# Half 0's products of six pairs instead of four ahead of the quarter sums, in the up projections of a two-layer trunk

## The chip, the core and the metric

The kernel runs on one core of one Trainium2 chip. The time is device microseconds of that core, the median of several executions; a profiled execution has a time of its own beside its span. The engines are PE (TensorE matmuls; PEld loads their weights beside it), DVE (VectorE), ACT (ScalarE), POOL (GpSimd) and SP (SyncE, which here only issues loads). In the trace each engine works off its instructions in the order in which they stand in the program, so what stands behind a waiting instruction on its engine is late with it.

## The reference, cut to what matters

```python
def squared_relu_mlp(h, w_up, w_down):
    return jnp.square(jax.nn.relu(h @ w_up)) @ w_down

# per layer, x is (1, 1024, 1024), w_up (1024, 4096), all float32
x = x + g_m[:, None, :] * rmsnorm(y, norm_g[l, 1])      # y: conv mixer (layer 0) or attention (layer 1)
h = modulate(rmsnorm(x, norm_g[l, 2]), sh_f, sc_f)
y = squared_relu_mlp(h, mlp_up_w[l], mlp_down_w[l])
x = x + g_f[:, None, :] * rmsnorm(y, norm_g[l, 3])
```

Two layers are computed, so there are two up projections. The change touches the place where the mixer's output projection ends, the residual `x` is written, `h` is formed, and the product `h @ w_up` begins.

## The kernel before, in words

**Numbers.** Each float32 operand is kept as a high part (`uphi`, the first tile of a pair, ACT's copy at L159) and a low part (`uplo`, DVE's subtraction at L160). A product of two such operands is three matmuls into one PSUM bank (`mm`, L156). Every matmul of the up projection is 128 by 128 by 512 tokens.

**The pairs.** The 4096 columns of `w_up` are taken in 16 pairs of 128-column blocks; with the tokens in two halves of 512 and the 1024 inner rows in two halves of four steps, a pair is a 2 by 2 block product, made by seven products instead of eight. Each product is 4 steps of 3 matmuls, 12 in all. On the tokens' side the seven operands are called `11` and `21` (half 0 of the tokens, inner rows 0 to 511 and 512 to 1023), `22` (from half 1), and `t1` to `t4` (sums over quarters of both halves). `11` and `21` need only half 0; the other five need half 1. On the weights' side a pair loads two blocks a and b: `11` and `21` use a as it is, and `pair_sums` (L467 on) forms `t2`, `s2` and `t3` from a and b, splitting each into high and low parts.

**The seam.** `Seam` closes the preceding projection, row tile by row tile: norm, gate, residual, store, norm again. `quarter_steps` then gives two lists. `steps0` holds eight steps for half 0: four transposes on PE into a `tp` bank and ACT's scaling at L374 (the front), then DVE's cast and subtraction at L384 and L385 (the back); they fill `11` and `21`. `steps1` holds four steps for half 1, one per quarter kk: eight transposes and two scalings (the front, `front1`), then the back, `back1`: four subtractions on DVE (L405, L407, L410, L412), five high parts on ACT (L395) and five low parts on DVE (L398). They fill `22` and `t1` to `t4`.

**`first_pairs`** writes by hand the order of work there; inside `with pinned()` each engine keeps the order in which the lines are written. It makes the two products of half 0 for the first AHEAD = 4 pairs (`first`: product 11, copied out of its bank by ACT at L599; `second`: product 21 on top of it, copied out with a Relu at L603), between the fronts and backs of `steps0` and `steps1`, and then the five other products of pair 0, one step kk of all five after the other. The weights of pairs 0 to 2 are split before, that of pair 3 (`late`) within.

**`all_pairs`** makes the other pairs. A pair whose half 0 is done already (called *begun* here: 1 to 3) has five products; any other has seven. Its last two products (`second` and `fourth` there) and the adds behind them are done within the next pair: behind the next pair's product 11 and product 21 if that pair is not begun, behind its first product of `s2` if it is. The second product into a bank has to wait until DVE has added the bank's value to its row (`take`, L528). Here the tile framework's scheduler sets the order on each engine. `sums` (L1124 to L1127) and the stores `ha` follow for each pair, and `load_pair` loads the next blocks into the four tiles of `raw`: a load waits until the tile's last reader, the split of `t3` two pairs before, is through.

## Time and profile before

| what | value |
| --- | --- |
| median of 3 runs (lowest to highest) | 2157.41 us (2154.37 to 2158.88) |
| the profiled execution: own time, span | 2159.2 us, 2157.4 us |
| busy share of the span: PE, DVE, ACT | 96%, 71%, 50% |
| 380 to 400 us: PE busy, granted clock | 17.57 of 20 us, 0.91 |
| 420 to 440 us: PE, DVE busy, granted clock | 14.17 and 18.75 of 20 us, 0.85 |
| 1550 to 1570 us: PE, DVE busy, granted clock | 14.19 and 18.27 of 20 us, 0.91 |

The first seam ends and the first up projection begins at about 385 us, the second at about 1510 us. A timeline row is the start in us, a duration in us, the engine, the line, the operation, output and inputs by name, the count of merged instructions, and in brackets the idle time ahead with what ended it. PE's matmuls are pipelined: one takes 0.39 us and the next starts 0.23 us after it. A waits row is the engine and line that waited, what it waited for, and us in total, times, and the longest.

### The profile page before, as it was taken

How to read it: one execution, taken by the hardware profiler on the slowest of the kernel's cores; microseconds unless marked ns; L12 is line 12 of the kernel's file. 1: busy time of each engine (PE TensorE's matmuls, PEld its weight loads, DVE VectorE, ACT ScalarE, POOL GpSimd, SP SyncE). 2: the span in 40 equal slices, each digit the busy share in tenths (PEclk: the TensorE clock that was granted, in tenths of full speed). 3: DMA queues.
4: the chain of work that ended last, by engine and by line, in shares of the span. 5: the costliest groups of instructions: out<-in, count | busy, mean ns of one | idle time of the engine just before them, and what ended most of it. 6: DMA issues, size and time to landing. Idle time of an engine off the chain costs nothing.

```text
span 2157.4 us, 25064 instructions
## 1 busy us (share of the span) xinstructions
PE 2062.0 (96%) x9438; PEld 1688.2 (78%) x9438; DVE 1541.2 (71%) x2087; ACT 1084.3 (50%) x1533; POOL 5.3 (0%) x13
## 2 busy tenths in 40 slices
PE   4999999989999999999899999999899999999998
PEld 3788878768888788888677788887678888788886
DVE  6877876876665669977688887756875665566576
ACT  4533353745554444455665565555744444544443
POOL 0000000000000000000000000000000000000000
PEclk9999999999999999999999999999999999999999
DMA  7444464254553889656223331143254653774355
GB/s 223 121 138 147 137 205 133 88 184 161 182 181 139 280 292 322 208 166 211 69 70 120 97 96 35 59 135 138 71 185 150 215 180 134 266 252 158 98 175 167
DMA packets 251023, 344.47 MB, mean 160 GB/s; under 512 B 19253, under 2 KB 142482, under 8 KB 250902
## 3 DMA queue, kind: packets, MB, share of 16 engines
q1 hardware_dynamic: 208408, 252.50, 37.4%
q10 hardware_dynamic: 42494, 90.38, 11.3%
q8 instruction: 74, 1.21, 0.2%
q14 instruction: 47, 0.39, 0.1%
HBM read 258.94 MB, written 83.89 MB: 159 GB/s over the span
## 4 chain that ended last, share of the span: by engine, by line
PE 77%; DVE 11%; ACT 6%; DMA 3%; issue 2%; ACTq 0%; SPq 0%; DVEq 0%
PE one L156 42%; PE mm L156 20%; PE tp L156 7%; PE big L156 3%; PE big L1360 2%; ACT junk L271 2%; DVE y L327 1%; PE tp L1386 1%; DVE raw L328 1%; DMA aw<-in_ada_w_dram 1%; ACT slot L1210 1%; DVE av L909 1%; PE tp L433 1%; DVE ring L160 1%; DVE acc L186 1%
## 5 line engine op out<-in xcount | busy, mean ns | idle before, releaser
L156 PE MATMUL one<-slot,uphi 128*128 128x512 f32 x1224 | 377.8, 389 | 0.0
L156 PEld LDWEIGHTS one<-slot,uphi 128*128 128x128 f32 x1224 | 230.4, 188 | 48.3 <-issue 0.5
L156 PE MATMUL one<-ring,ring 128*128 128x512 f32 x1152 | 262.9, 389 | 2.3 <-DVE ring L160 2.3
L160 DVE TENSOR_TENSOR uplo<-raw,uphi 128x1024 fp32r<-128x1024 f32 x127 | 153.3, 1222 | 143.1 <-ACT uphi L159 143.1
L156 PEld LDWEIGHTS one<-ring,ring 128*128 128x128 f32 x1152 | 215.9, 188 | 48.3 <-ACT ring L159 3.1
L156 PE MATMUL one<-slot,uplo 128*128 128x512 f32 x612 | 240.7, 393 | 8.2 <-DVE y L528 3.8
L160 DVE TENSOR_TENSOR ring<-raw,ring 128x1024 fp32r<-128x1024 f32 x144 | 174.3, 1220 | 55.6 <-ACT ring L159 55.3
L159 ACT ACTIVATE ring<-raw 128x1024 fp32r<-128x1024 f32 x144 | 149.5, 1052 | 106.6 <-DMA raw<-ha 61.6
L159 ACT ACTIVATE uphi<-raw 128x1024 fp32r<-128x1024 f32 x127 | 134.7, 1061 | 118.6 <-PE one L156 82.3
L156 PE MATMUL mm<-ring,ring 128*128 128x512 f32 x768 | 185.0, 390 | 1.6 <-DVE ring L160 1.6
L156 PE MATMUL tp<-ring,ring 128*128 128x512 f32 x768 | 183.9, 389 | 0.0
L159 ACT ACTIVATE ring<-w 128x1024 fp32r<-128x1024 f32 x80 | 84.8, 1060 | 178.7 <-PE tp L156 102.7
L156 PEld LDWEIGHTS mm<-ring,ring 128*128 128x128 f32 x768 | 143.7, 188 | 32.1 <-DVE ring L160 2.5
L156 PEld LDWEIGHTS tp<-ring,ring 128*128 128x128 f32 x768 | 144.1, 188 | 29.9
L160 DVE TENSOR_TENSOR ring<-w,ring 128x1024 fp32r<-128x1024 f32 x80 | 97.8, 1222 | 81.1 <-ACT ring L159 81.1
L156 PEld LDWEIGHTS one<-slot,uplo 128*128 128x128 f32 x612 | 115.2, 188 | 35.8 <-DVE y L528 5.5
L186 DVE SCALAR_TENSOR_TENSOR acc<-raw,csil,acc 128x1024 f32<-128x1024 f32 x88 | 112.5, 1278 | 22.8 <-DMA raw<-in_ada_w_dram 18.0
L526 ACT ACTIVATE y<-one 128x512 f32<-128x512 f32 x66 | 39.0, 591 | 159.6 <-PE one L156 118.5
L156 PE MATMUL mm<-slot,uphi 128*128 128x512 f32 x344 | 109.2, 399 | 9.6 <-DVE slot L398 9.4
L156 PE MATMUL one<-slot,s 128*128 128x512 f32 x468 | 112.9, 390 | 1.1 <-DVE s L160 1.1
L156 PEld LDWEIGHTS one<-slot,s 128*128 128x128 f32 x468 | 87.6, 188 | 20.6 <-DVE s L160 2.4
L156 PE MATMUL one<-q,uphi 128*128 128x512 f32 x328 | 101.9, 392 | 0.0
(267 smaller groups left out, 3614.4 us busy)
## 6 DMA issues: line engine op xcount, KB each, us to landing
ha<-y ACTq DMA_DIRECT2D x224, 256.0 KB, 4.0
raw<-ha SPq DMA_DIRECT2D x112, 512.0 KB, 4.0
raw<-in_ada_w_dram SPq DMA_DIRECT2D x80, 512.0 KB, 4.3
raw<-in_mlp_up_w_dram SPq DMA_DIRECT2D x70, 512.0 KB, 4.5
w<-in_mlp_down_w_dram SPq DMA_DIRECT2D x48, 512.0 KB, 7.0
raw<-in_mlp_down_w_dram SPq DMA_DIRECT2D x32, 512.0 KB, 4.0
raw<-in_conv_in_w_dram SPq DMA_DIRECT2D x18, 512.0 KB, 4.1
xs<-raw ACTq DMA_DIRECT2D x18, 512.0 KB, 2.8
```

Source lines behind the costliest of these rows:

```text
L156: nc.tensor.matmul(out_, lhs[a], rhs[b], start=first and i == 0, stop=last and i == 2, skip_group_check=more)
L159: nc.scalar.activation(hi, src, AF.Copy)
L160: nc.vector.tensor_tensor(lo, src, hi.bitcast(F32), op=ALU.subtract)
L186: nc.vector.scalar_tensor_tensor(acc, raw, s, acc, op0=ALU.mult, op1=ALU.add)
L271: nc.scalar.activation(junk, src, AF.Square, accum_out=ss)
L327: nc.vector.scalar_tensor_tensor(y, y, rroot(ss), self.gmb, op0=ALU.mult, op1=ALU.mult)
L328: nc.vector.tensor_tensor(xr, xr, y, op=ALU.add)
L433: nc.tensor.transpose(p_[:, t * P:(t + 1) * P], ys[half * 4 + t][:, k * P:(k + 1) * P], ident)
L526: nc.scalar.activation(dst, x_, AF.Copy)
L909: nc.vector.scalar_tensor_tensor(acc, raw[:, i, :], csil[:, i:i + 1], acc, op0=ALU.mult, op1=ALU.add)
L1210: nc.scalar.activation(y[32 * i:32 * i + 32, :], p_[32 * j:32 * j + 32, :], AF.Copy, scale=scale)
L1360: nc.tensor.matmul(o_, a, m_, start=j == 0, stop=j == 4)
```

## The change

AHEAD becomes 6, so products 11 and 21 of pairs 4 and 5 also move from `all_pairs` into `first_pairs`, and `first_pairs` is written anew. Both products' PSUM tiles come from two of the same four banks (`one`). The rows of pairs 4 and 5, and the raw blocks of their weights, share two tiles in a new pool `ex`, which also holds one buffer for the split of pair 3's weights; those two blocks are loaded a second time by `load_pair` later. Product 11's copy (`keep`) is now apart from the product (`first`). The fronts and backs of half 1 stand at other places, one front of half 0 moves from the last row tile into `first_pairs`, and the first call of `pair_sums` comes after more of the products of half 0. The five last products of pair 0 are no longer broken by anything. `between` keeps its old bound of 8. Lines up to the old L456 have a number one higher in the new kernel (L156 is L157, L398 is L399, L528 is L529); `keep` is L610, `second`'s copy L614, and `sums` begins at L1151.

```diff
-AHEAD = 4
+AHEAD = 6
+READY = 3
...
-                    self.front(steps, 2)
+                    self.front(steps, 2 if t < 7 else 1)
...
-        tiles = [mm_ps(), mm_ps(), bank_ps(), bank_ps()]
-        ca = [row_tile() for _ in range(AHEAD)]
-        late = ad.tile([P, D], F32, tag="acc", name=nm("w"), bufs=1).rearrange("p (k m) -> p k m", k=KD)
-        ld(late, wmat[:, 2 * (AHEAD - 1) * P:(2 * AHEAD - 1) * P].rearrange("(k p) m -> p k m", p=P))
+        ex = ar[3]
+        tiles = [mm_ps(), mm_ps()] + [bank_ps() for _ in range(AHEAD - 2)]
+        ca = [row_tile() for _ in range(4)]
+        late = [ad.tile([P, D], F32, tag="acc", name=nm("w"), bufs=1)]
+        late += [ex.tile([P, D], F32, tag="ahead", name=nm("ahead"), bufs=AHEAD - 4) for _ in range(AHEAD - 4)]
+        for i, raw in enumerate(late, READY):
+            ld(raw.rearrange("p (k m) -> p k m", k=KD), wmat[:, 2 * i * P:(2 * i + 1) * P].rearrange("(k p) m -> p k m", p=P))
+        ca += late[1:]
+
+        def ready():
+            i = len(ws) - READY
+            ws.append(up_split(up if i else ex, late[i].rearrange("p (k m) -> p k m", k=KD), bufs=3 if i else 1))

         def first(i):
             prod(tiles[i], (ws[i], 0, "11"), ops)
+
+        def keep(i):
             nc.scalar.activation(ca[i][:, HALF:], tiles[i], AF.Copy)
...
-        a, b = load_pair(wmat, 0)
+        def back1():
+            seam.backs.pop(0)()
+
         with pinned():
             first(0)
             seam.back()
             seam.front(steps0, 2)
             first(1)
+            seam.flush()
             seam.back()
-            seam.flush()
-            second(0)
-            ws.append(up_split(up, late))
-            sums = pair_sums(up, a, b)
-            next(sums)
-            second(1)
-            next(sums)
-            seam.front(steps1, 1)
-            rest = next(sums)
+            seam.front(steps0, 1)
+            ready()
+            seam.back()
+            keep(0)
+            keep(1)
             first(2)
             seam.front(steps1, 1)
-            seam.backs.pop(0)()
+            first(3)
+            keep(2)
+            keep(3)
+            second(0)
+            back1()
+            ready()
+            seam.front(steps1, 1)
+            sums = pair_sums(up, *load_pair(wmat, 0))
+            second(1)
+            ready()
             second(2)
+            next(sums)
+            first(4)
+            keep(4)
+            next(sums)
+            first(5)
+            keep(5)
+            back1()
+            seam.front(steps1, 1)
+            second(3)
+            rest = next(sums)
+            second(4)
+            back1()
+            seam.front(steps1, 1)
+            second(5)
             rest.update(next(sums))
-            first(3)
-            seam.front(steps1, 1)
-            seam.backs.pop(0)()
+            back1()
             out_ = {6: mm_ps(), 5: mm_ps(), 3: bank_ps(), 7: bank_ps(), 4: bank_ps()}
             for kk in range(4):
                 for j in (5, 6, 4, 3, 7):
                     prod(out_[j], rest[j], ops, kks=[kk])
-                if kk == 0:
-                    second(3)
-                    seam.front(steps1, 1)
-                if kk < 2:
-                    seam.backs.pop(0)()
...
+        ar.append(pool("ex"))
...
-            if i >= 2 * AHEAD:
+            if i >= PAIRS // 2:
```

What this moves is seen in the order of the instructions. Names: `slot` and `q` with a number are the operands 22 and t1 to t4 (one quarter each, or one row of them), `s` is the weight sum s2, `raw` half 1 of the tokens or a weight block, `sums` a quarter sum, `y` and `ahead` the rows of a pair's results.

First the split of `t3` for pair 0 on ACT. Before, it (`uphi_3194`) stands behind the first quarter's high parts, ahead of the scalings of the third quarter:

```order
L395 ACTIVATE slot_2262<-raw_3120 128x512 [waits DVE_49]
L395 ACTIVATE q_3175<-sums_3165 128x512 [waits DVE_49]
L603 ACTIVATE y_3027<-one_3023 128x512 [waits PE_49]
L159 ACTIVATE uphi_3194<-raw_3031 128x1024 [waits DMAHW7_49]
L599 ACTIVATE y_3028<-one_3024 128x512 [waits PE_49]
L374 ACTIVATE raw_3211<-tp_3212,v_2428,v_2424 128x512 [waits DMAHW0_49,PE_49,Activation_49]
```

Now (`uphi_3347`) it stands behind the third quarter's high parts, the fourth quarter's scalings and the copy of the last product of pair 5:

```order
L396 ACTIVATE slot_2248<-raw_3260 128x512 [waits Activation_49]
L396 ACTIVATE slot_2263<-sums_3305 128x512 [waits DVE_49]
L396 ACTIVATE slot_2252<-raw_3260 128x512 [waits DVE_49]
L396 ACTIVATE slot_2262<-raw_3260 128x512 [waits DVE_49]
L396 ACTIVATE q_3315<-sums_3305 128x512 [waits DVE_49]
L375 ACTIVATE raw_3321<-tp_3322,v_2431,v_2427 128x512 [waits PE_49]
L375 ACTIVATE raw_3321<-tp_3328,v_2431,v_2427 128x512 [waits PE_49]
L614 ACTIVATE ahead_3030<-one_3023 128x512 [waits PE_49]
L160 ACTIVATE uphi_3347<-raw_3178 128x1024 [waits DMAHW5_49]
```

Second, ACT where the first quarter of half 1 is split, in the new kernel: its first high part (`slot_2246`) stands behind the copies of product 11 of pairs 2 and 3 and of product 21 of pair 0:

```order
L610 ACTIVATE y_3026<-one_3020 128x512
L610 ACTIVATE y_3027<-one_3021 128x512 [waits PE_49]
L614 ACTIVATE y_3024<-mm_3018 128x512 [waits PE_49]
L396 ACTIVATE slot_2246<-raw_3105 128x512 [waits Activation_49]
L396 ACTIVATE slot_2263<-sums_3145 128x512 [waits DVE_49]
```

Before, the same high part stood behind the scalings of two quarters and behind product 11's copy of pair 2 only.

Third, DVE in pair 3. Before, the second `take` of pair 3 (the second L528, `y_3575<-y_3028`) has ahead of it the split and the first difference of pair 4's blocks (`raw_3659`), which wait for their load; pair 4 is not begun:

```order
L548 TENSOR_TENSOR y_3027<-y_3027,one_3453 128x512 [waits PE_49]
L160 TENSOR_TENSOR uplo_3572<-raw_3554,uphi_3571 128x1024 [waits Activation_49]
L1124 TENSOR_TENSOR y_3619<-y_3027 128x512 [waits DMAHW7_49,DMAHW6_49,Activation_49]
L554 TENSOR_TENSOR y_3470<-y_3470,one_3527 128x512 [waits PE_49]
L160 TENSOR_TENSOR uplo_3666<-raw_3659,uphi_3665 128x1024 [waits DMAHW3_49,Activation_49]
L1125 TENSOR_TENSOR y_3027<-y_3027,y_3470 128x512 [waits DVE_49,Activation_49]
L474 TENSOR_TENSOR raw_3659<-raw_3659,raw_3661 128x512 [waits DMAHW4_49,DVE_49]
L1126 TENSOR_TENSOR y_3619<-y_3027 128x512 [waits DVE_49]
L528 TENSOR_TENSOR y_3575<-y_3028,one_3558 128x512 [waits PE_49]
```

Now pair 4 is begun too, and ahead of pair 3's second `take` (L529, `y_3644<-y_3027`) stand the first difference of pair 5's blocks (`raw_3833`), which waits for their load, a split of pair 4's and three more:

```order
L549 TENSOR_TENSOR y_3026<-y_3026,one_3522 128x512 [waits PE_49]
L161 TENSOR_TENSOR uplo_3641<-raw_3623,uphi_3640 128x1024 [waits Activation_49]
L1151 TENSOR_TENSOR y_3688<-y_3026 128x512 [waits DMAHW1_49,DMAHW2_49,DVE_49,Activation_49]
L555 TENSOR_TENSOR y_3539<-y_3539,one_3596 128x512 [waits PE_49]
L475 TENSOR_TENSOR raw_3833<-raw_3833,raw_3835 128x512 [waits DMAHW7_49,DMAHW6_49,DVE_49]
L161 TENSOR_TENSOR uplo_3736<-raw_3730,uphi_3735 128x1024 [waits Activation_49]
L1152 TENSOR_TENSOR y_3026<-y_3026,y_3539 128x512 [waits DVE_49,Activation_49]
L480 TENSOR_TENSOR raw_3730<-raw_3730,raw_3728 128x512 [waits DVE_49]
L1153 TENSOR_TENSOR y_3688<-y_3026 128x512 [waits DVE_49]
L529 TENSOR_TENSOR y_3644<-y_3027,one_3627 128x512 [waits PE_49]
```

`raw_3833` lies in the tile of `raw_3623`, whose last reader is the split of pair 3's `t3` four rows above it (`uplo_3641`). The second up projection has the same order at all three places. On SP the two loads into `ex` stand far ahead: in layer 0 among the loads of the conv mixer's weights (one just ahead, one just behind the second block of its third product group), where the first waits for PE's last use of that memory; in layer 1 between the loads of the attention output's fourth and fifth rows of weights, where the first waits for the attention's last use.

More of the change, by code (lines that the diff above doesn't have):

```diff
@@ L454, in up_weights, with up_split @@
         return up_split(up, r3, kk)
-    def up_split(up, r3, kk=KD):
-        hi = up.tile([P, KD, P], F32R, tag="uphi", name=nm("uphi"), bufs=3)
-        lo = up.tile([P, KD, P], F32R, tag="uplo", name=nm("uplo"), bufs=3)
+    def up_split(up, r3, kk=KD, bufs=3):
+        hi = up.tile([P, KD, P], F32R, tag="uphi", name=nm("uphi"), bufs=bufs)
+        lo = up.tile([P, KD, P], F32R, tag="uplo", name=nm("uplo"), bufs=bufs)
         split_w(hi[:, :kk, :], lo[:, :kk, :], r3[:, :kk, :])
@@ L648, in release_arena @@
     def release_arena():
-        for q in (ar[2], ar[1], ar[0]):
+        for q in ar[::-1]:
             q.release()
@@ L1097, in down_phase @@
         steps0, steps1 = quarter_steps(ys, key, hs)
-        wcols = [next_w[:, 2 * i * P:(2 * i + 1) * P] for i in range(AHEAD - 1)]
+        wcols = [next_w[:, 2 * i * P:(2 * i + 1) * P] for i in range(READY)]
         down(slots, sizes, wd, src_fn, ys, seam, steps0, 0, lambda: ws.extend(up_weights(up, [w]) for w in wcols), begun)
```

## The prediction

> **What bounds the kernel now.** I read the page first, then the table by stretches around both seams, the waits of PE there, and the timelines of PE, DVE and ACT.
>
> ```profile
> span 2157.4 us, 25064 instructions
> PE 2062.0 (96%) x9438; PEld 1688.2 (78%) x9438; DVE 1541.2 (71%) x2087; ACT 1084.3 (50%) x1533; POOL 5.3 (0%) x13
> ...
> core 0: us, PE busy (x) PEld busy (x) DVE busy (x) ACT busy (x) POOL busy (x), PEclk, DMA share, GB/s
> ...
> 420.00:440.00 20.00, 14.17 (x57) 10.84 (x57) 18.75 (x30) 10.54 (x17) 0.00 (x0) 0.85 0.29 81
> 440.00:460.00 20.00, 19.01 (x80) 15.01 (x80) 16.82 (x26) 10.70 (x12) 0.00 (x0) 0.98 0.61 202
> ```
>
> PE is the bound of the program; only where it idles can a new order gain. Around the seam it idles in one stretch, and there DVE is the busy engine, 18.75 of 20 us. The waits of PE from 380 to 440 us, and from 440 to 520 us:
>
> ```profile
> PE mm L156 <- DVE slot L398: 4.7, 2, 3.2
> PE tp L373 <- ACT q L374: 2.2, 2, 1.2
> PE mm L156 <- ACT slot L395: 1.2, 1, 1.2
> PE one L156 <- ACT y L599: 1.1, 1, 1.1
> ...
> PE one L156 <- DVE y L528: 1.9, 2, 1.1
> PE one L156 <- DVE s L160: 0.2, 1, 0.2
> ```
>
> So 9.2 us of waits up to the end of pair 0 and 2.1 us in the begun pairs 1 to 3. The largest stand in pair 0's five products, where PE takes the quarters faster than DVE finishes them, and the matmuls behind the longest run slowly:
>
> ```profile
> 428.20 0.73 PE L156 MATMUL mm<-slot,uphi 128*128 128x512 f32 x2 [1.42 <-DVE slot L398]
> ...
> 432.82 0.51 PE L156 MATMUL mm<-slot,uplo 128*128 128x512 f32 x1 [1.17 <-ACT slot L395]
> 436.57 1.22 PE L156 MATMUL mm<-slot,uphi 128*128 128x512 f32 x2 [3.24 <-DVE slot L398]
> 437.58 1.48 PE L156 MATMUL mm<-slot,s 128*128 128x512 f32 x3
> ...
> 441.88 2.89 PE L156 MATMUL one<-slot,s 128*128 128x512 f32 x12
> 444.62 0.39 PE L156 MATMUL one<-slot,uplo 128*128 128x512 f32 x1
> ```
>
> A product of 12 takes 2.74 us (441.88 to 444.62), 0.23 a matmul. The second seam answers it, here from 1515 to 1580 us:
>
> ```profile
> PE mm L156 <- DVE slot L398: 4.7, 2, 3.3
> ```
>
> So all is counted once and doubled.
>
> **The change, part by part.** No arithmetic is added: 48 matmuls per projection (two pairs, 24 each) move from pairs 4 and 5 to before pair 0's block. That is 4 x 2.74 = 11 us more of PE's work ahead of the block. Does DVE catch up meanwhile? These rows price its work, one quarter's back and one split:
>
> ```profile
> 416.00 1.22 DVE L160 TENSOR_TENSOR uplo<-raw,uphi 128x1024 fp32r<-128x1024 f32 x1
> 417.13 0.69 DVE L405 TENSOR_TENSOR sums<-raw 128x512 f32<-128x512 f32 x1
> 417.86 0.69 DVE L407 TENSOR_TENSOR raw<-raw,q 128x512 f32<-128x512 f32 x1
> 418.46 0.69 DVE L398 TENSOR_TENSOR slot<-raw,slot 128x512 fp32r<-128x512 f32 x1
> 419.18 0.69 DVE L410 TENSOR_TENSOR raw<-raw 128x512 f32<-128x512 f32 x1
> 419.91 0.69 DVE L412 TENSOR_TENSOR sums<-q,raw 128x512 f32<-128x512 f32 x1
> ...
> 422.32 0.69 DVE L398 TENSOR_TENSOR q<-sums,q 128x512 fp32r<-128x512 f32 x1
> 423.05 0.69 DVE L405 TENSOR_TENSOR sums<-raw 128x512 f32<-128x512 f32 x1
> ...
> 415.09 1.03 PE L373 MATMUL tp<-cs,y 128*128 128x128 f32 x8
> 415.88 0.48 PE L156 MATMUL mm<-slot,uplo 128*128 128x512 f32 x1
> ```
>
> A quarter costs DVE 5.92 us (417.13 to 423.05), its L412 ends 3.5 us after its start, a split costs 1.13, a short operation 0.6, and eight transposes cost PE 0.79. On ACT:
>
> ```profile
> 414.24 0.58 ACT L603 ACTIVATE y<-one 128x512 f32<-128x512 f32 x1
> 414.72 1.05 ACT L159 ACTIVATE uphi<-raw 128x1024 fp32r<-128x1024 f32 x1
> ...
> 416.15 1.45 ACT L374 ACTIVATE raw<-tp,v,v 128x512 f32<-128x512 f32 x2
> 417.47 0.64 ACT L395 ACTIVATE slot<-raw 128x512 fp32r<-128x512 f32 x1
> ```
>
> *The block of pair 0.* I run both sides from the end of pair 0's product 21. PE has, in its new order: three times eight transposes (2.4), seven products (19.1: 21 of pairs 1 to 5, 11 of pairs 4 and 5), then nine matmuls of the block (2.0) until the first that needs t3: 23.5 us. DVE cannot go on with the first quarter at once, as its first high part stands on ACT behind the copy of that product 21: 0.6 + 0.6 us. Then 4.6 us for the rest of that quarter, to 5.8; the split of pair 4's block, to 7.0, for which PE waits (product 11 of pair 4 is due at 0.8 + 2 x 2.74 = 6.3): a new wait of 0.8, so PE arrives at 24.3. Pair 5's split, two sums and t2's split with their high parts on ACT in between (t2's high part stands behind product 11's copy of pair 4: 9.9 + 0.6, and takes 1.05) bring DVE to 12.7; the second quarter to 18.6; s2 with its high part on ACT 2.5, to 21.1. The third quarter's L412 then ends at 24.6. Now ACT: its last high part (0.5), two scalings (1.35), pair 5's copy (0.5), t3's high part (1.05), to 28.0; DVE's split 1.22, to 29.2. PE waits 29.2 - 24.3 = 4.9 us in one piece. By then the fourth quarter follows in time. The three waits of 1.42, 1.17 and 3.24 (5.8) become one of 4.9: a gain of 0.9. The cover of 11 us is eaten by two splits and, above all, by DVE standing idle behind ACT's copies at the start and t3's split coming last instead of early.
>
> *The rest of the front.* The wait for L599's copy (1.1) goes, since several products now lie between. Against it stand the 0.8 above and the split of pair 3's block, whose high part now stands behind pair 0's last scalings: between 0 and one split's 1.05 on ACT, and I take 0.3, since product 11 of pair 2 and eight transposes lie in between. The two waits of transposes for L374 (2.2) are made by half 0's scalings and stay. Sum: -0.9 - 1.1 + 0.8 + 0.3 = **-0.9 us** per seam; bounds -9 (no wait left) and +1.
>
> *The begun pairs.* Five of them follow one another now. In each the second product into a bank waits for DVE's L528:
>
> ```profile
> 451.00 0.50 PE L156 MATMUL one<-slot,uplo 128*128 128x512 f32 x1 [0.78 <-DVE y L528]
> ...
> 466.53 0.50 PE L156 MATMUL one<-slot,uplo 128*128 128x512 f32 x1 [1.13 <-DVE y L528]
> ```
>
> These are pairs 1 and 2. Pair 3 shows none, since the products 11 and 21 of pair 4 (5.5 us of PE) lay between; the change takes these away, and pairs 3 and 4 are open too. By order DVE has, ahead of pair 3's second `take`, the first difference of pair 5's blocks, whose load starts only when the split of pair 3's t3 has read the tile. The prices:
>
> ```profile
> L160 DVE TENSOR_TENSOR uplo<-raw,uphi 128x1024 fp32r<-128x1024 f32 x12 | 14.5, 1223 | 8.5 <-ACT uphi L159 8.5
> ...
> raw<-in_mlp_up_w_dram SPq DMA_DIRECT2D x10, 512.0 KB, 4.3
> ```
>
> From PE's end of the previous pair's `second` product: t3's high part 1.05 (as above), its split 1.22, the load 4.3, the difference 0.6, a split 1.13, three short ones 1.8, `take` 0.69: 10.8 us. PE has in that time the previous `fourth` and two products, 3 x 2.74 = 8.2. Wait: **2.6**, with some semaphores 2.8. Pair 4 has a split of pair 5's in that place and no load: between 1.1 (pair 2's) and 2.8, I take 1.8. Pair 1 begins later than its DVE work allows: its s2 low part stands behind pair 2's first difference, which also waits for a load; between 0.2 (the s row) and 2.8, I take 1.4. Pairs 1 and 2 keep 0.8 and 1.1, the latter with a load ahead of it as well, to 1.4. Sum 1.4 + 0.8 + 1.4 + 2.8 + 1.8 = 8.2 against 2.1: **+6.1** per seam; bounds +2 (two more like pair 2's) and +10 (2.8 in each).
>
> *Loads.* Two blocks more per projection. The memory is last used, and SP has its gap, as here:
>
> ```profile
> L156 PE MATMUL one<-slot,w x48: 389/389/389, 102.8 to 117.5; 128*128 128x512 f32 x48
> ...
> L1422 ACTq DMA_DIRECT2D hd<-o x4: 326/326/327, 1386.4 to 1427.5; - x4
> ...
> 1401.84 0.33 SPq L114 DMA_DIRECT2D raw<-hd  x1
> 1432.86 0.33 SPq L114 DMA_DIRECT2D raw<-in_attn_o_w_dram  x1
> ```
>
> In layer 0 the use ends long before the loads' place; in layer 1 it ends inside a gap of 31 us on SP. Zero; without that gap up to 5 us.
>
> *The clock.* After the 3.24 us wait two matmuls take 1.01 us (436.57 to 437.58) instead of 0.46; until 441.88 the order has 14, which is 3.2 us of work in 5.3: a loss of 2.1. A wait of 4.9 us pays it again, so it cancels against the one of before. Whether a wait of 2.8 us pays it too no row quoted here decides; the bounds are 0 and 2.1 per seam, and I take 0, since the waits of 1.42 and 1.17 us paid none (428.20 has its usual 0.73 for two). [...]
>
> **The sum.** Per seam -0.9 + 6.1 = +5.2, both +10.4. From the profiled execution's 2159.2 us that gives 2169.6. This execution was 1.8 above the median of 2157.4, so I state 2167.8: **2168 us**, 0.5% slower.
>
> **The rivals.**
>
> *Slower still* (2172 to 2180): the loads land later than 4.3 us as five begun pairs in a row move the same bytes in less time, each 0.5 us costing it in three pairs, +1.5 per seam, and pair 3's wait cools the clock, +2 per seam: 2175. For it: the 61% DMA share of the begun pairs. Against: landings there are steady at 4.3.
>
> *Balance* (2154 to 2162): the begun pairs cost only +2 each seam, and the front gains 2 as DVE gets ahead a little sooner: 2157. It decides if pair 3's load is issued a few us sooner than I chained it.
>
> *Faster* (2138 to 2150): DVE keeps up, the block's 5.8 us and its 2 us of slow clock vanish, -9 with the copy's 1.1, and the begun pairs cost +2: -7 per seam, 2143. One mechanism: t3's split not held by ACT's order. It decides if DVE does the run above in 24 us instead of 29. For it: 11 us of cover. Against: the order puts t3 behind the third quarter.
>
> *It doesn't do what it says*: the pairs do move by the order, so only a held SP queue could undo it (above), no more than 3 in 100, within "slower still".
>
> **How the numbers follow.** My forecast (2163 to 2172) gets 0.60, slower still 0.17, balance 0.13, faster 0.10. About 0.2% (4.3 us) is what a measurement of this kernel tells from no change. Balance reaches into all three, mostly "same". Faster 0.11, same 0.13, slower 0.76. The range, 2156 to 2178, leaves out the faster case and the top of the slower one.
>
> **What would show it.** In the new profile: one wait of 4 to 5.5 us of PE for L161 (t3's split) in pair 0's block near 437 us, with no L399 wait behind it; waits of PE for L529 that sum to 6 to 9 us in the 75 us after it, the longest in pair 3; no wait for L610. Wrong would be: a block without any wait over 2 us, or begun pairs with 3 us in all.

## The result, and the profile after

The changed kernel takes 2175.47 us (median of 4 runs, 2173.62 to 2178.19) against 2156.96 us for the kernel before, run beside it: a ratio of 1.008, 95% interval 1.0063 to 1.0096. Run again beside the first experiments it has 1.0066 (1.0053 to 1.0078). It is slower by 14.1 to 18.5 us; the forecast was 2168 us, slower by 10.6.

The head of the page after:

```profile
span 2173.6 us, 25063 instructions
PE 2066.3 (95%) x9438; PEld 1690.7 (78%) x9438; DVE 1546.3 (71%) x2095; ACT 1077.8 (50%) x1525; POOL 5.6 (0%) x13
```

PE has the same 9438 matmuls and is busy 4 us longer with them. To see where the time went, both executions are cut at the first transposes of each seam. The timeline of PE before, and then after:

```profile
372.91 0.49 PE L373 MATMUL tp<-cs,y 128*128 128x128 f32 x3
...
1496.05 0.49 PE L373 MATMUL tp<-cs,y 128*128 128x128 f32 x3
```

```profile
374.11 0.49 PE L374 MATMUL tp<-cs,y 128*128 128x128 f32 x3
...
1504.79 0.49 PE L374 MATMUL tp<-cs,y 128*128 128x128 f32 x3
```

From seam to seam it is 1123.1 us before and 1130.7 after, and from the second seam to the end of the span 661.4 and 668.8: **+7.6 and +7.4 us, one seam like the other**. The stretch ahead of the first seam, in which only the two early loads are new, differs by 1.2. A second profile of the changed kernel has +6.7 and +8.1. So the change costs about 7.5 us per seam, where the sum had 5.2.

The waits of PE after, from 370 to 440 us and from 440 to 530 us:

```profile
PE one L157 <- DVE uplo L161: 5.5, 3, 4.6
PE tp L374 <- ACT q L375: 1.7, 2, 1.0
...
PE one L157 <- DVE y L529: 9.1, 4, 4.0
```

and in the timeline of PE the places where they stand:

```profile
437.02 0.80 PE L157 MATMUL one<-slot,uplo 128*128 128x512 f32 x1 [4.64 <-DVE uplo L161]
...
460.19 0.50 PE L157 MATMUL one<-slot,uplo 128*128 128x512 f32 x1 [1.16 <-DVE y L529]
...
476.37 0.50 PE L157 MATMUL one<-slot,uplo 128*128 128x512 f32 x1 [2.28 <-DVE y L529]
...
479.24 3.80 PE L157 MATMUL one<-slot,s 128*128 128x512 f32 x12
...
495.94 0.79 PE L157 MATMUL one<-slot,uplo 128*128 128x512 f32 x1 [4.04 <-DVE y L529]
...
499.95 3.70 PE L157 MATMUL one<-slot,s 128*128 128x512 f32 x12
...
514.12 0.50 PE L157 MATMUL one<-slot,uplo 128*128 128x512 f32 x1 [1.61 <-DVE y L529]
```

The three waits in pair 0's block have become one, for t3 (437.02), and each of the pairs 1 to 4 now waits for its second `take`: 9.1 us where there were 1.9. Before, all waits of PE from 370 to 530 us sum to 11.3 us, after to 16.8: +5.5 of the +7.6. In the second seam, from 1490 to 1670 us, they sum to 11.7 and 18.0: +6.3 of the +7.4. What is left, 2.1 and 1.1 us, goes with matmuls at a low granted clock (0.50 from 477.74 to 481.15 and from 494.81 to 501.63 us): a product of twelve, usually 2.74 us from first to last start, needs 3.64 behind the wait of 2.28 us (479.24 to 482.88), and 3.5 behind that of 4.04.

Behind the wait of 4.04 us stands a load, as DVE's and SP's timelines show:

```profile
484.86 1.22 DVE L161 TENSOR_TENSOR uplo<-raw,uphi 128x1024 fp32r<-128x1024 f32 x1 [0.41 <-ACT uphi L160]
...
491.66 0.69 DVE L475 TENSOR_TENSOR raw<-raw,raw 128x512 f32<-128x512 f32 x1 [3.91 <-DMA raw<-in_mlp_up_w_dram]
...
495.21 0.68 DVE L529 TENSOR_TENSOR y<-y,one 128x512 f32<-128x512 f32 x1
```

```profile
486.11 0.37 SPq L115 DMA_DIRECT2D raw<-in_mlp_up_w_dram  x1
```

The split of t3 (484.86) frees the tile, SP issues the load for pair 5 at 486.11, DVE's first difference on it starts at 491.66, and the take for which PE waits (L529, 495.21) stands behind it, a split and three short operations later.

In front of the block DVE stands idle at one place for 4.5 us. ACT's and then DVE's timeline:

```profile
407.77 0.60 ACT L614 ACTIVATE y<-mm 128x512 f32<-128x512 f32 x1 [2.13 <-PE mm L157]
408.26 0.62 ACT L396 ACTIVATE slot<-raw 128x512 fp32r<-128x512 f32 x1
```

```profile
403.74 0.69 DVE L408 TENSOR_TENSOR raw<-raw,q 128x512 f32<-128x512 f32 x1
408.92 0.69 DVE L399 TENSOR_TENSOR slot<-raw,slot 128x512 fp32r<-128x512 f32 x1 [4.49 <-ACT slot L396]
```

The first quarter's high part (L396) stands on ACT behind the Relu copy of pair 0's product 21 (L614), which itself waits for PE; DVE, which has just started that quarter, waits with it. So there are three suspects: the load chain in the begun pairs, DVE's idle time in front (or t3's place in the order, which the prediction named beside it as a cause of the block's wait), and the low clock.

### The profile page after: what moved, and what is told of

It reads as the page before. It is cut to its first block, busy times and chain, and to the rows that moved or that the text cites. A ratio compares the mean times of both kernels' runs of the same rounds, so it can differ in the third digit from the quotient of the medians.

```text
span 2173.6 us, 25063 instructions
## 1 busy us (share of the span) xinstructions
PE 2066.3 (95%) x9438; PEld 1690.7 (78%) x9438; DVE 1546.3 (71%) x2095; ACT 1077.8 (50%) x1525; POOL 5.6 (0%) x13
## 4 chain that ended last, share of the span: by engine, by line
PE 73%; DVE 13%; ACT 7%; DMA 4%; issue 2%; ACTq 0%; SPq 0%; DVEq 0%
PE one L157 38%; PE mm L157 19%; PE tp L157 7%; PE big L157 4%; PE big L1387 2%; ACT junk L272 2%; DMA raw<-in_mlp_up_w_dram 1%; DVE y L328 1%; PE tp L1413 1%; DVE raw L329 1%; DVE uplo L161 1%; ACT slot L1237 1%; ACT uphi L160 1%; DVE slot L399 1%; DVE av L935 1%
## 5 line engine op out<-in xcount | busy, mean ns | idle before, releaser
L157 PE MATMUL one<-slot,uphi 128*128 128x512 f32 x1256 | 392.0, 394 | 0.0
L157 PE MATMUL one<-slot,uplo 128*128 128x512 f32 x628 | 250.8, 399 | 31.4 <-DVE y L529 18.1
L157 PEld LDWEIGHTS one<-slot,uphi 128*128 128x128 f32 x1256 | 239.0, 190 | 49.6 <-issue 0.5
L157 PE MATMUL one<-ring,ring 128*128 128x512 f32 x1152 | 262.9, 390 | 2.3 <-DVE ring L161 2.3
L157 PEld LDWEIGHTS one<-ring,ring 128*128 128x128 f32 x1152 | 215.9, 188 | 48.3 <-ACT ring L160 3.1
L161 DVE TENSOR_TENSOR uplo<-raw,uphi 128x1024 fp32r<-128x1024 f32 x123 | 148.7, 1221 | 129.3 <-ACT uphi L160 129.3
L161 DVE TENSOR_TENSOR ring<-raw,ring 128x1024 fp32r<-128x1024 f32 x144 | 174.2, 1219 | 54.6 <-ACT ring L160 54.1
L160 ACT ACTIVATE uphi<-raw 128x1024 fp32r<-128x1024 f32 x123 | 130.3, 1060 | 139.8 <-PE one L157 76.8
L157 PE MATMUL mm<-ring,ring 128*128 128x512 f32 x768 | 185.0, 390 | 1.4 <-DVE ring L161 1.4
L157 PE MATMUL tp<-ring,ring 128*128 128x512 f32 x768 | 183.9, 389 | 0.0
L157 PEld LDWEIGHTS one<-slot,uplo 128*128 128x128 f32 x628 | 119.1, 190 | 63.8 <-DVE y L529 22.2
L157 PEld LDWEIGHTS mm<-ring,ring 128*128 128x128 f32 x768 | 143.7, 188 | 31.8 <-DVE ring L161 2.3
L157 PEld LDWEIGHTS tp<-ring,ring 128*128 128x128 f32 x768 | 144.1, 188 | 29.8
L161 DVE TENSOR_TENSOR ring<-w,ring 128x1024 fp32r<-128x1024 f32 x80 | 97.6, 1220 | 83.3 <-ACT ring L160 82.6
L157 PE MATMUL one<-slot,s 128*128 128x512 f32 x468 | 114.9, 395 | 0.7 <-DVE s L161 0.7
L157 PEld LDWEIGHTS one<-slot,s 128*128 128x128 f32 x468 | 89.8, 192 | 20.4 <-DVE s L161 1.3
L527 ACT ACTIVATE y<-one 128x512 f32<-128x512 f32 x58 | 34.3, 592 | 141.1 <-PE one L157 107.3
L157 PE MATMUL one<-q,uphi 128*128 128x512 f32 x328 | 101.0, 389 | 0.0
L157 PE MATMUL mm<-slot,uphi 128*128 128x512 f32 x312 | 97.0, 392 | 0.6 <-DVE slot L386 0.4
```

What stands on the lines that cost most here:

```text
L157: nc.tensor.matmul(out_, lhs[a], rhs[b], start=first and i == 0, stop=last and i == 2, skip_group_check=more)
L160: nc.scalar.activation(hi, src, AF.Copy)
L161: nc.vector.tensor_tensor(lo, src, hi.bitcast(F32), op=ALU.subtract)
L527: nc.scalar.activation(dst, x_, AF.Copy)
```

## The experiments

Ratios are to the kernel before on the same chip, with the 95% interval. "Seam 1" and "seam 2" are the two stretches cut as above, as differences from the profile of the kernel before (1123.1 and 661.4 us); the two profiles of the changed kernel differ there by 0.9 and 0.7 us.

| run | median us | ratio | seam 1, seam 2 |
| --- | --- | --- | --- |
| e1 changed kernel again | 2171.15 | 1.0066 (1.0053 to 1.0078) | +6.7, +8.1 |
| e2 take first | 2157.38 | 1.000 (0.999 to 1.0009) | +1.0, -0.2 |
| e3 one dummy in the block | 2167.24 | 1.0048 (1.0035 to 1.006) | +4.8, +4.8 |
| e4 twelve dummies in the block | 2166.98 | 1.0049 (1.0036 to 1.0062) | +5.2, +4.5 |
| e5 t3 early | 2179.24 | 1.0097 (1.0082 to 1.0111) | +11.3, +11.5 |
| e6 front order | 2155.08 | 0.998 (0.997 to 0.9989) | +1.5, +0.5 |
| e7 front order and take first | 2141.27 | 0.992 (0.9906 to 0.9933) | -8.2, -7.8 |
| e8 four begun | 2165.5 | 1.003 (1.0019 to 1.0041) | +3.1, +3.8 |
| e9 one dummy in pair 3 | 2170.3 | 1.0066 (1.0054 to 1.0079) | +4.8, +8.5 |
| e10 fourteen dummies in pair 3 | 2169.5 | 1.0058 (1.0045 to 1.007) | +7.9, +5.6 |
| e11 four with both | 2151.7 | 0.9972 (0.9963 to 0.9981) | -2.9, -2.8 |

### The changed kernel again (e1)

No edit.

> The changed kernel once more, beside the other three on one chip. Expected: 2173 to 2178 us and 1.007 to 1.009 times the kernel before. Every theory says the same; it is the base of the three next comparisons.

2171.15 us, ratio 1.0066: a little under what was expected. It is the base of what follows.

### The take ahead of the late difference (e2)

```diff
-            for part in pair_sums(up, ra, rb):
+            n = len(bb.instructions)
+            for i, part in enumerate(pair_sums(up, ra, rb)):
                 rest.update(part or {})
+                if i == 0 and len(takes) > 1 and takes[-2] is not None:
+                    tc.add_manual_dep(bb.instructions[n], takes[-2], NO_SYNC, reason="after take")
...
             take(u4)
+            takes.append(None if p1 is None else bb.instructions[-1].name)
```

> The changed kernel, in which the first difference of the blocks of pair k+2 (L475), which waits for a load, may stand on DVE only behind the second take (L529) of begun pair k; no instruction is added. Theory one, the load chain (the take waits behind a load that is not its own): the waits of 2.28 us in pair 2 and 4.04 us in pair 3 shrink to 0.7 and 1.7 us, so -3.9 us per seam, and with them go the slow matmuls behind them (after 476.37 12 matmuls in 3.64 us instead of 2.74, after 495.94 21 in 7.55 instead of 4.8): another 2 to 4 us per seam. Sum -12 to -16: 2159 to 2164 us, nearly the kernel before. Theory two, DVE has simply too much to do with five begun pairs in a row: the waits only move to the next pairs' low parts, 2172 to 2176 us. If the load chain is right but slow matmuls cost nothing: 2167 to 2169 us.

2157.38 us, 14 us below the changed kernel: the load chain's full sum (a little under the range named, as the changed kernel was). The line of the take is L533 here. The waits of PE from 440 to 530 us, and the stretch that had a clock of 0.84 in the changed kernel:

```profile
PE one L157 <- DVE y L533: 4.0, 3, 1.6
...
480.00:500.00 20.00, 17.91 (x78) 14.14 (x76) 13.77 (x20) 9.06 (x10) 0.00 (x0) 1.00 0.63 210
```

Pair 2 has no wait over 0.3 us left, pair 3 has 1.60. From the last transposes of the seam to the first product of pair 6 PE now needs 97.6 us instead of 106.8 (the profile of the changed kernel above, 426.57 to 533.32 us; here 422.78 to 520.34): -9.2, of which -5.1 are waits (9.1 to 4.0). The remaining 4.1 go with the slow matmuls in the begun pairs, which are gone (the granted clock of that stretch is 1.00). The loads are the same, but no instruction of DVE waits for one there any more (L475 starts without a wait at 472.25 and at 487.87 us), since it now runs later than the take. DVE has neither more work nor less, so the theory that five begun pairs are too much for DVE falls.

### Dummies inside the block's wait (e3, e4)

```diff
                 for j in (5, 6, 4, 3, 7):
+                    if kk == 0 and j == 3:
+                        warm = tp_ps()
+                        for i in range(WARM):
+                            nc.tensor.matmul(warm, rest[6][0][0][:, i % 4, :], ops["t2"][0][0], start=i == 0, stop=i == WARM - 1)
                     prod(out_[j], rest[j], ops, kks=[kk])
```

WARM is 1 in e3 and 12 in e4.

> The changed kernel with one matmul into a bank of the transposes, which nothing reads, ahead of the first product of pair 0's block that uses t3. It waits for ACT to read the last transposes, so the wait of 4.64 us is cut in two pieces of about 1.5 and 3 us. It is the control of the next run; the order of DVE's work behind the block also moves a little (the takes of pairs 1 and 2 stand earlier), by which both may be 2 to 6 us below the changed kernel: 2168 to 2175 us by every theory.

> The same with twelve such matmuls (2.74 us of PE inside the wait) and, but for them, the same order on every engine. Theory three, the slow clock costs time of its own: the wait for t3 shrinks to under 1 us, the 8 to 10 matmuls behind it run at 0.23 us instead of 0.42, and PE's end of the block lies 2 us earlier in each seam: 3 to 5 us below the run with one dummy. Rival, the clock's loss is hidden, since DVE sets the time behind the block: within 1 us of the run with one dummy.

With one dummy 2167.24 us, with twelve 2166.98: no difference. The timelines of PE, first with one dummy, then with twelve:

```profile
433.46 0.76 PE L158 MATMUL one<-slot,uplo 128*128 128x512 f32 x1 [2.86 <-DVE uplo L162]
...
455.86 0.50 PE L158 MATMUL one<-slot,uplo 128*128 128x512 f32 x1 [0.78 <-DVE y L530]
```

```profile
430.59 3.02 PE L667 MATMUL tp<-slot,s 128*128 128x512 f32 x12 [1.29 <-ACT raw L376]
433.95 0.50 PE L158 MATMUL one<-slot,uplo 128*128 128x512 f32 x1 [0.34 <-DVE uplo L162]
...
446.65 3.01 PE L158 MATMUL one<-slot,s 128*128 128x512 f32 x12 [0.80 <-DVE s L162]
...
455.88 0.50 PE L158 MATMUL one<-slot,uplo 128*128 128x512 f32 x1 [0.78 <-DVE y L530]
```

The dummies did keep the clock (the granted clock from 420 to 440 us is 1.00 instead of 0.91 with one, and the matmul after the wait takes 0.50 instead of 0.76). PE is then ahead, and waits 0.80 us for pair 1's `s2`, which it did not wait for with one dummy. From t3's split to pair 1's take it is 22.4 us with one and 21.9 with twelve: of the 2 us that the expectation reckons for the slow clock behind the block 0.5 are gained. There DVE sets the time. Both runs lie 4 us under the changed kernel, since the takes of pairs 1 and 2 stand earlier on DVE in both; pair 3's wait is as before.

### t3 early (e5)

```diff
-        t3 = up_split(up, a)
+        t3 = up_split(last, a, bufs=1) if last else up_split(up, a)
...
-            sums = pair_sums(up, *load_pair(wmat, 0))
+            sums = pair_sums(up, *load_pair(wmat, 0), ex)
...
             rest = next(sums)
+            rest.update(next(sums))
             second(4)
...
             second(5)
-            rest.update(next(sums))
             back1()
```

> The changed kernel, in which pair 0's t3 is split into a buffer of its own right behind s2, ahead of the fourth product 21, and no longer behind the third quarter. Theory of the prediction (t3's place at the end of ACT's and DVE's order makes the wait of the block): the wait of 4.64 us shrinks to under 2 us and the slow matmuls behind it go; where DVE sets the time behind the block that may not be kept whole: 2165 to 2171 us. Rival, DVE is behind by that much whatever comes first: the wait leaves t3 and comes back in the block's last quarter and, with 4 to 6 us, in pair 1's s2, which now stand behind; the time stays, 2170 to 2178 us.

2179.24 us, 1.0097: not faster than the changed kernel, which has 1.008 and 1.0066 on other occasions. The waits from 370 to 530 us:

```profile
PE one L157 <- DVE y L529: 9.3, 3, 3.9
PE one L157 <- DVE s L161: 6.2, 1, 6.2
...
PE mm L157 <- DVE slot L399: 1.1, 1, 1.1
```

The wait for t3 is gone, and one of 6.2 us for pair 1's `s2` has come, with 1.1 for the block's last quarter. t3's place alone was not the cause; DVE is behind by that much, whatever comes first.

### The written order of the front (e6)

```diff
             ready()
             seam.back()
-            keep(0)
-            keep(1)
             first(2)
+            keep(0)
             seam.front(steps1, 1)
-            first(3)
+            sums = pair_sums(up, *load_pair(wmat, 0))
             keep(2)
-            keep(3)
-            second(0)
             back1()
+            first(3)
+            keep(3)
+            keep(1)
+            second_(0)
             ready()
...
             rest = next(sums)
-            second(4)
+            second_(3)
+            keep(5)
+            relu(1)
+            relu(2)
+            relu(0)
             back1()
-            seam.front(steps1, 1)
-            second(5)
+            second_(4)
+            relu(3)
             rest.update(next(sums))
...
```

`second_` is the product alone, `relu` its copy out of the bank (L614 of the changed kernel).

> The changed kernel with another written order from the first product to pair 0's block: the same calls, but the high parts and backs of the quarters and the splits stand ahead of ACT's copies that must wait for a product of PE (the copies of the six pairs come later, the Relu copies last). DVE stands idle for 4.5 us behind such a copy in the changed kernel (the first quarter's L399 behind L614's copy) and 0.7 to 1.3 us at four more places, 8 in all. Theory four, this idle time of DVE is the block's wait: the wait for t3 (4.64 us) falls under 1 us, and 4.5 to 6 us per seam are gained: 2160 to 2166 us. Rival, DVE's work alone fills the front, and the time saved is lost behind the block: over 2169 us. The load chain in pairs 2 and 3 stays in both.

2155.08 us, 0.998: by the ratios 18 us below the changed kernel (1.0066), and just under the kernel before. The waits of PE from 370 to 530 us:

```profile
PE one L157 <- DVE y L529: 7.8, 4, 2.6
...
PE one L157 <- DVE s L161: 0.6, 1, 0.6
...
PE one L157 <- DVE uplo L161: 0.3, 1, 0.3
```

The block has no wait left (5.5 us before for L161, now 0.3), and DVE's longest idle stretch from 395 to 450 us is 1.13 us instead of 4.49. Beside e1 the seams are 5.2 and 7.6 us shorter: that wait with one of 0.6 ahead of it, and 1.3 us in the begun pairs (7.8 instead of 9.1). These 13 us are less than the medians' 18; the profiled execution was 5 us over its median. So the block's wait goes when DVE no longer stands idle behind ACT's copies. The edit also takes t3, the sums and the load of pair 0's blocks forward; t3's place alone gained nothing (e5), the other two were not moved by themselves.

### Both (e7)

The edits of e2 and e6 together.

> Both: the written order of the front, and the second take ahead of the difference that waits for a load. If the two causes are apart, the gains add: 14 us of the take and 9 to 12 of the front, 2144 to 2150 us, below both kernels (0.994 to 0.997 of the kernel before). If a gain in front is given back at the next wait of the begun pairs: 2153 to 2158 us.

2141.27 us, 0.992 (0.9906 to 0.9933) of the kernel before: faster than both kernels, and faster than expected. DVE goes through the first quarter at once (L408 at 399.36, its neighbour L399 at 399.97), and the waits from 370 to 530 us are 7 us in all:

```profile
399.36 0.69 DVE L408 TENSOR_TENSOR raw<-raw,q 128x512 f32<-128x512 f32 x1
399.97 0.69 DVE L399 TENSOR_TENSOR slot<-raw,slot 128x512 fp32r<-128x512 f32 x1
```

```profile
PE one L157 <- DVE y L533: 3.6, 3, 1.6
PE tp L374 <- ACT q L375: 1.7, 2, 1.0
PE one L157 <- DVE s L161: 0.9, 1, 0.9
```

Against the changed kernel the two cures are worth 14 and 18 us alone and 31 together (0.992 against 1.0066), so they add: two causes, not one that moves. The profiles agree, with 31 us in the two seams of e7 against e1 (14.9 and 15.9). Not all of it is waiting: the waits of the first seam went from 16.6 us in e1 to 7, and the granted clock of e7 is 1.00 in every 20 us from 380 to 540 and from 1520 to 1660 us.

### Four begun pairs in the new arrangement (e8), and with both cures (e11)

```diff
-AHEAD = 6
+AHEAD = 4
...
-            ready()
...
-            ready()
...
-            first(4)
-            keep(4)
...
-            first(5)
-            keep(5)
...
-            second(4)
...
-            second(5)
```

> The new arrangement (banks, copies, quarters ahead of the sums, the third block in the pool apart) with four begun pairs, as before the change: pair 4 and 5's products are back behind pair 3. By the prediction's sum the begun pairs are those of before again (2 to 3 us of waits in pairs 1 to 3, no slow clock there), and the block lacks 11 us of cover: its waits grow from 5 to 9 to 13 us in all. Expected 2164 to 2172 us, over before and under the changed kernel. If the cover is what the change gains in the block, its waits stand 5 us above those of the changed kernel; if the cover is worth nothing (DVE starves with it), they stay at 5 to 6 us and the time falls to 2155 to 2160 us.

> Four begun pairs in the new arrangement, with the written order of the front that has the backs and splits ahead of ACT's copies, and the second take ahead of the late difference. It tells what six pairs are worth once both causes are gone. If the 11 us of cover let DVE catch up in front: a wait of 4 to 7 us for t3 comes back in pair 0's block, with a slow clock behind it, and the time is 5 to 12 us over that of six pairs with both (0.992 of the kernel before): 2147 to 2154 us. If the cover is worth nothing: 2139 to 2144 us.

Without the cures four pairs take 2165.5 us (1.003), 0.36% under six; with them 2151.7 us (0.9972), 0.5% over six with them. The waits from 370 to 530 us of four pairs, without and then with the cures:

```profile
PE one L157 <- DVE uplo L161: 6.8, 2, 6.5
PE tp L374 <- ACT raw L375: 4.2, 1, 4.2
...
PE one L157 <- DVE y L529: 1.2, 1, 1.2
```

```profile
PE one L157 <- DVE uplo L161: 5.4, 2, 5.1
...
PE one L157 <- DVE s L161: 1.4, 1, 1.4
PE one L157 <- DVE y L533: 0.8, 1, 0.8
```

Four pairs have 11.0 us of waits in and ahead of the block (6.8 and 4.2) where six have 5.5: the cover of 11 us of matmuls is worth 5.5 us. In the begun pairs it is 1.2 against 9.1. So the two further pairs gain in front and give more back behind. Of the 0.66% that the changed kernel loses, the new arrangement with four pairs already loses 0.30%, and the two further pairs the other 0.36%. With both cures six pairs have no wait for t3, four still 5.1: then the cover is a clear gain.

### Dummies inside pair 3's wait (e9, e10)

```diff
-            def second(x_=x_, rest=rest):
+            def second(x_=x_, rest=rest, third=begun is not None and len(takes) == 3):
+                if third:
+                    warm = tp_ps()
+                    for i in range(WARM):
+                        nc.tensor.matmul(warm, rest[5][0][0][:, i % 4, :], ops["t1"][0][0], start=i == 0, stop=i == WARM - 1)
                 prod(x_, rest[3], ops, False)
```

WARM is 1 in e9 and 14 in e10.

> The changed kernel with one matmul, which nothing reads, into a bank of the transposes, from the tiles of pair 3's product 5, ahead of pair 3's product that waits for the take behind the late difference. The control of the next run: the waits of 2.28 us (pair 2) and 4.04 us (pair 3) stay within 0.3 us, the time within 2 us of the changed kernel: 2170 to 2177 us.

> The same with fourteen such matmuls; by the order on PE four of them stand in pair 2's wait and ten in pair 3's (0.9 and 2.3 us), which leaves idle stretches of 1.4 and 1.7 us. Theory three, the slow clock behind these two waits costs time of its own (1.3 us after the first, 2.8 us after the second, by the slow rows): no matmul behind them is slow, and the time is 4 to 8 us below the run with one dummy. Rival, as in pair 0's block: DVE and the load set the time behind these waits too, and what PE saves is waited for again: within 1.5 us of the run with one dummy.

2170.3 and 2169.5 us, with intervals that overlap: by the times a gain of 8 us is excluded, and one between 0 and 4 is not decided. The profiles say why: the dummies kept the clock in the second seam (1.00 from 1610 to 1630 us against 0.83 with one) and failed to in the first (0.91 from 480 to 500 us with either). Pair 3 in the second seam, with one dummy and then with fourteen, and last the first seam with fourteen:

```profile
1620.28 0.80 PE L158 MATMUL one<-slot,uplo 128*128 128x512 f32 x1 [3.76 <-DVE y L530]
...
1624.29 3.53 PE L158 MATMUL one<-slot,s 128*128 128x512 f32 x12
```

```profile
1620.85 2.43 PE L548 MATMUL tp<-slot,uphi 128*128 128x512 f32 x10
1625.03 0.50 PE L158 MATMUL one<-slot,uplo 128*128 128x512 f32 x1 [1.75 <-DVE y L530]
1626.84 3.06 PE L158 MATMUL one<-slot,s 128*128 128x512 f32 x12
```

```profile
492.59 0.50 PE L158 MATMUL one<-slot,uplo 128*128 128x512 f32 x1 [1.78 <-DVE y L530]
...
495.01 3.79 PE L158 MATMUL one<-slot,s 128*128 128x512 f32 x12
```

Where the clock was kept, the stretch from the seam's first transposes to the first product of pair 6 is 156.9 us (1503.09 to 1660.01) instead of 158.8 (1498.64 to 1657.48): 1.9 us. Where it was not, nothing is gained (104.4 against 104.1 from the last transposes to pair 6). A second place by chance: with one dummy pair 2's wait in the first seam is 2.05 us with no slow matmul behind it (nine matmuls from 473.28 to 475.46, 2.18 us), in the changed kernel run beside e2 it is 2.29 with slow matmuls behind it (the same nine from 473.29 to 476.91, 3.62 us). From the last transposes to pair 6 that is 104.1 against 106.4 us, but the block's low clock differs there too; from the end of pair 2's wait it is 54.1 (473.28 to 527.40) against 55.7 (473.29 to 528.96). So one fall of the clock in the begun pairs costs 1.6 to 1.9 us in these profiles, other than in the block. It rests on single profiles, and the times do not show it on their own.

## Why the prediction was right or wrong

**Direction and mechanism: right.** Slower was forecast, and 2168 us with a range to 2178; it came out at 2175 and, the second time, at 2171. What was named to be seen was seen: one wait of PE for L161 in pair 0's block (4.64 us at 437.02, between the 4 and 5.5 given, 4.9 in the sum), no wait behind it for L399, none for L610, and waits for L529 of 9.1 us (6 to 9 named), the longest in pair 3.

**The block and the front: the size right, the cause half wrong.** From 370 to 440 us the waits went from 9.2 to 7.7 us, -1.5 where -0.9 was reckoned: t3 4.6 (4.9), pair 4's split 0.60 (0.8), pair 3's 0.31 (0.3), the transposes 1.7 (2.2 kept). The prediction gave, beside two splits, two reasons for the 4.9: DVE idle behind ACT's copies, and "t3's split coming last instead of early", the latter as the one that decides its faster rival. e5 put t3 early, and the wait went to pair 1's `s2` and grew; e6 took DVE's idle time away, and it vanished. So the first reason carries the wait, and the second alone does not. The sum came out since it ran along the order as it stood; the rival's condition ("t3's split not held by ACT's order") was the wrong one. Without DVE's idle time, and with the take ahead as well, the faster case does exist: e7, at 2141.

**The begun pairs: +7.0 instead of +6.1.** The chain in pair 3 was right, link by link, and undersized: 2.8 us forecast, 4.04 measured. The load is the link that was late: issued at 486.11, used at 491.66, 5.5 us instead of the 4.3 taken from the median ("steady at 4.3"; from 440 to 530 us the median to landing rose from 4.3 to 4.8). Pair 2 has 2.28 (1.4), again a load in front of its take. Pair 4, without a load, 1.61 (1.8). Pair 1's take 1.16 (0.8), and its `s2`, priced 1.4 between 0.2 and 2.8, waits for nothing. e2 shows the chain to be the cause: with the same load and the same work, and the take ahead of it, those two waits are 1.6 together instead of 6.3. A slip in the bounds: 2.8 us in each of the five terms, less 2.1, is 11.9, not the 10 stated.

**The clock: the term that failed.** "The bounds are 0 and 2.1 per seam, and I take 0." At the block's wait of 4.64 us the granted clock is 0.50 from 436.78 to 440.19 us, and at the 3.24 us before it was 0.50 from 434.08 to 440.90: paid in both, as reckoned. But at the waits of 2.28 and 4.04 us in the begun pairs, and of 3.84 in the second seam, it is 0.50 as well: three times in that profile (from 477.74, 494.81 and 1624.62 us; at the wait of 2.18 us in pair 2 of the second seam it stays at 1.00). Beside the waits 2.1 and 1.1 us are left in the two seams: the upper bound in one, half of it in the other. With the upper bound the sum is 2172. It also left out that the clock was low in front before: PE does not idle "in one stretch" only, and the clock is 0.54 from 392.86 to 396.27 us and 0.50 from 1512.70 to 1516.10. After the change there is no low clock in front (1.00 from 380 to 436 and from 1503 to 1566 us), so what is left is the difference of a loss in the begun pairs and a smaller gain in front.

The prediction took its 0 from the waits of 1.42 and 1.17 us, of which its rows show no price. 2.28 us did have one and so did, in e10, 1.78 us (twelve matmuls in 3.79 us behind it), while 2.18 us had none: one place, pair 2's wait, was slow in one seam and not in the other (the last section has the rows).

What e3 and e4 add is that a low clock had a price only where PE sets the time: 0.5 us of 2 behind the block, where DVE does, 1.6 to 1.9 in the begun pairs.

**Loads: zero, and nothing here speaks against it.** No wait for a load of the two added blocks appears in front.

**The rivals.** The first measurement, 2175, lies within "slower still", the second, 2171, within the forecast, and the reasons are those of the former: the load later than 4.3 us, and a low clock at pair 3's wait. "Balance" and "faster" did not come by themselves; e2 at 2157 and e7 at 2141 have their times, and needed another order on DVE or ACT.

## What to carry to other kernels

When work is moved away from a place, look at what it covered there: pairs 4 and 5's products hid pair 3's take behind a load, and no table of the place they were moved to shows that. On an engine that works in order, as DVE and ACT do here, an operation that waits for something slow (a load on DVE, a PE-paced copy on ACT) delays everything written behind it; ask of each long idle stretch what stands next in line and whether it could go first, before adding cover. A low clock behind a wait was paid here only where PE was the one that others wait for (1.6 to 1.9 us, against 0.5 of 2 where DVE was).

## What was not expected of the hardware

How long PE idles does not alone decide here whether the clock falls. In the changed kernel 2.28 us at 476.37 is followed by slow matmuls (the product of twelve takes 3.80), 2.18 us at the same place of the second seam is not (1608.61 us; a product of twelve there takes its 2.9). The granted clock shows the same. In the block and the begun pairs of that profile's first seam it stands at half from 436.78, 477.74 and 494.81 us on, the first two times for 3.41 us and the last for twice that, and these starts lie 12 and 5 times 3.41 us apart. So the trace is cut here into stretches of 3.41 us on that beat. The rows give a stretch and its length, then busy us (and instructions) of PE, PEld, DVE, ACT and POOL, the granted clock, and DMA's share and GB/s:

```profile
474.33:477.74 3.41, 1.37 (x6) 1.15 (x7) 3.41 (x7) 0.63 (x1) 0.00 (x0) 1.00 0.41 154
477.74:481.15 3.41, 3.41 (x10) 2.64 (x9) 0.38 (x1) 0.00 (x0) 0.00 (x0) 0.50 0.68 208
...
1604.14:1607.55 3.41, 2.29 (x11) 1.55 (x9) 3.41 (x6) 0.00 (x0) 0.00 (x0) 1.00 0.42 156
1607.55:1610.96 3.41, 2.35 (x10) 1.94 (x11) 2.80 (x5) 0.63 (x1) 0.00 (x0) 1.00 0.62 231
```

The wait of 2.28 us lies with 2.04 us in one stretch, in which PE is busy for 1.37 us, and the next is at half clock; the wait of 2.18 us is shared out over two stretches, busy 2.29 and 2.35 us, and the clock stays. Slow matmuls begin later than PE resumes: PE resumes at 476.37, the half clock starts at 477.74. In the block and the begun pairs of the two profiles, of the kernel before and of the changed one, seven full-clock stretches have 1.50 us or less of PE, and behind each the clock is at half (before: 1.50 us from 430.66 and 0.51 from 1557.06; after: 0.00 from 433.37, 1.37 from 474.33, 0.50 from 491.40, 1.16 from 1563.18 and 1.35 from 1621.21); the others have 1.80 us or more, and behind none of them it is. So in these two profiles a wait counted by how much of it fell into one such stretch, and that shifts with everything ahead of it. For the front, with its transposes, this was not worked out.
